# Turning the keys of both forgetting heads of a pair in one transpose, after the last scores of the pair in front

## Chip, cores and metric

The kernel runs on one core of a Trainium2 chip. The metric is the device time of one execution in microseconds (us), the median of three runs. The engines are TensorE (PE; its weight loads are shown apart as PEld), VectorE (DVE), ScalarE (ACT), GpSimd (POOL) and SyncE (SP), whose queue issues the DMAs.

## What is computed

One decoder layer over 1024 positions of width 1024 in float32. An input projection of the normalised x feeds two groups of eight heads of 64: group A, attention in a sliding window with sinks, and group B, "forgetting" attention, which is causal softmax attention with a bias from cumulated log gates. Both go through an output projection, and a feed-forward part follows.

```
xn = rmsnorm(x, attn_norm_g)
qa, ka, va, qb, kb, vb, f_logit = split(xn @ w_in)
out_a = swa_sinks_attention(rmsnorm(qa), rmsnorm(ka), va, sink_logits)
log_f = log_sigmoid(f_logit + b_forget);  c = cumsum(log_f)
# forgetting attention, for each head
sc = rmsnorm(qb) @ rmsnorm(kb).T / 8 + c[t] - c[s]      (s <= t)
out_b = softmax(sc) @ vb
x = x + concat(out_a, out_b) @ w_out
x = x + square(relu(rmsnorm(x) @ w_up)) @ w_down
```

## The kernel before

Each float32 product is done in three matmuls of float32r parts: a value is cast to a high part, and the rest is kept as a low part. Queries and keys are stacked: `q1` holds the high part of a head's query in its 64 rows and the low part in the other 64, `k1` holds the high part of the key in both row halves, and `k2` the low part of the key (`k2_of[h]`, one tile for each of the two heads of a pair, with zeros in the other rows). So the scores are two matmuls, q1 by k1 and q1 by k2.

Group B is worked in four pairs of heads, p = 0 to 3. The projection of pair p (`project_b`, eight row tiles of 24 matmuls each, tile `ps`) writes `qkb[p]`, rows of positions with columns for queries (128), keys (128) and values (128) of the two heads, and normalises them in place on POOL (`qknorm`, L239). For the scores the queries and keys have to be turned, so that positions are columns. `turn` (L299) takes four 128 x `w` blocks through PE into one PSUM tile `pt`, one of three with the tag "tr"; the same three serve the probabilities (`tpb`, L705). A half c of the positions is 512 columns.

`make_k_b` (L360) turns the keys of one head: for each half four transposes of 64 columns (`ptk`), then `k_split` (L341): two casts on ACT (L343, L344, into both row halves of k1) and one subtraction on DVE (L346, into `k2z`). For the sliding heads `make_k_a` (L352) takes 128 columns at once, two heads in one `pt`, and splits them one after the other. Queries of B are turned for both heads at once as well (`make_q_b`, `ptq`).

The pair runs in eight units u: u = 0 to 3 are head 0 and u = 4 to 7 head 1, over the query blocks in the order (0, 2, 1, 3), in which block qp has 2 qp + 2 key blocks of 128. A unit is `scores_b` (PE matmuls `spb`, a DVE reduction that adds the bias row `cb`, an exponential on ACT) and, two units later, `mix_b` (transposes `tpb`, a cast `pth` on ACT and a subtraction `ptl` on DVE for each block of 256 keys, matmuls `pvb`, an addition `mtb`). Between units `ahead(p + 1, u)` prepares the next pair: queries after u = 4, keys of head 0 and the load of its bias row after u = 5, values after u = 6, keys of head 1 after u = 7. `k1` tiles rotate through two places, `q1` tiles through four.

The order of instructions on each engine is worked out at compile time by a list scheduler over a simulated timeline, in which `prep(...)` gives high priority; projections (`fillers`) have low priority and may start only behind the scores of a certain unit (PACE, `issue_after`). After pair 3's projection its weights and the input make room for the output projection (`out_start`): `mix` tiles are loaded back from DRAM, weights `wor` are split into `wos`, and the products of the first half of `w_out` (`out_first`, tile `po`) are the fillers from then on.

Of the kernel before, what the change touches and what calls it, by code (L numbers as in the profile page):

```python
# [8 lines left out]
F32 = mybir.dt.float32  # L9
F32R = mybir.dt.float32r  # L10
# [6 lines left out]
P = 128  # L17
D = 1024
S = 1024
KT = D // P  # L20
NT = S // P
HD = 64
# [33 lines left out]
def hybrid_layer(  # L56
# [13 lines left out]
    nc = tc.nc  # L70
# [74 lines left out]
    ap2 = at.enter_context(tc.tile_pool(name="ap2", bufs=1, side="right"))  # L145
# [147 lines left out]
    def q_split(hi, lo, src, gain):  # L293
        nc.scalar.activation(hi, src, AF.Copy, scale=gain)
        nc.vector.scalar_tensor_tensor(
            out=lo, in0=src, scalar=gain, in1=hi.bitcast(F32), op0=ALU.mult, op1=ALU.subtract
        )

    def turn(x, col, w, c, name):  # L299
        pt = pa.tile([P, 512], F32, tag="tr", name=name, bufs=3)  # L300
        for j in range(4):
            nc.tensor.transpose(  # L302
                pt[:w, j * P : (j + 1) * P], x[:, 4 * c + j, col : col + w], ident
            )
        return pt
# [3 lines left out]
    def paced():  # L309
        return tc.issue_after(marks[-1]) if marks else nullcontext()  # L310

    qa, va = {}, []
    rows_of = [slice(h * HD, (h + 1) * HD) for h in range(2)]

    def tiles_q_a(g, c):
        for j in range(2):
            qa[g, j, c] = ap2.tile([P, 2, 512], F32R, tag="q1", name=f"q1a{g}{j}", bufs=4)

    def make_q_a(g, c, j):
        x, col = (((q0, 0), (q3, 0)), ((q3, P), (q3, 2 * P)))[g][j]  # L320
# [4 lines left out]
            q_split(q1[r, h, :], q1[ro, h, :], pt[r, :], gqk[r, 0:1])  # L325

    def make_q_b(x, p):
        q1 = [ap2.tile([P, S], F32R, tag="q1", name=f"q1b{p}{h}", bufs=4) for h in range(2)]
        for c in range(2):
            cs = slice(c * 512, (c + 1) * 512)  # L330
            pt = turn(x, 0, P, c, "ptq")
            for h in range(2):
                r, ro = rows_of[h], rows_of[1 - h]
                q_split(q1[h][r, cs], q1[h][ro, cs], pt[r, :], gqk[r, 1:2])
        return q1
# [3 lines left out]
    k2_of = [ap2.tile([P, S], F32R, name=f"k2z{i}") for i in range(2)]  # L339

    def k_split(k1, i, src, cs, both):  # L341
        r, ro = rows_of[i], rows_of[1 - i]
        nc.scalar.copy(k1[r, cs], src)  # L343
        nc.scalar.copy(k1[ro, cs], src)  # L344
        for rr in (r, ro) if both else (r,):
            nc.vector.tensor_tensor(  # L346
                out=k2_of[i][rr, cs], in0=src, in1=k1[r, cs].bitcast(F32), op=ALU.subtract
            )

    k1a = {}  # L350

    def make_k_a(x, col, c):  # L352
        cs = slice(c * 512, (c + 1) * 512)
        pt = turn(x, col, P, c, "ptk")
        for g in range(2):
            if c == 0:
                k1a[g] = ap2.tile([P, S], F32R, tag="k1", name=f"k1a{g}", bufs=2)
            k_split(k1a[g], g, pt[rows_of[g], :], cs, True)

    def make_k_b(x, col, p, h):  # L360
        k1 = ap2.tile([P, S], F32R, tag="k1", name=f"k1b{p}{h}", bufs=2)
        if p == 0:
            nc.gpsimd.memset(k2_of[h][rows_of[1 - h], :].bitcast(F32), 0.0)
        for c in range(2):
            cs = slice(c * 512, (c + 1) * 512)
            pt = turn(x, col + h * HD, HD, c, "ptk")
            k_split(k1, h, pt[:HD, :], cs, False)
        return k1

    def evict_pt(pt, cols):  # L370
        hi = ap2.tile([P, 512], F32R, tag="pth", name="pth", bufs=3)
# [107 lines left out]
    def start_a():  # L479
        for c in range(2):  # L480
            tiles_q_a(0, c)
        for t in range(2):
            wa1_tile(t)
        for c in range(2):
            wa1_tile(2 + c)
            with tc.issue_after(middle[-1]):
                prep(make_k_a, q0, P, c)
            prep(make_q_a, 0, c, 0)
        for g in range(2):
            va.append(split_v(q0[:, :, 256 + g * HD : 256 + (g + 1) * HD], f"va{g}"))  # L490
        prep(make_q_a, 0, 0, 1)
        for t in range(4, NT):
            wa1_tile(t)
        prep(make_q_a, 0, 1, 1)
# [128 lines left out]
    heads = {}  # L623

    def prep_q(p):
        heads[p, "q"] = make_q_b(qkb[p], p)

    def prep_k(p, h):
        heads[p, "k1", h] = make_k_b(qkb[p], P, p, h)
        if h == 0:  # L630
            load_c(p, 0)

    def load_c(p, h):
        cb = heads[p, "cb", h] = ap2.tile([P, S], F32, tag="bias", name=f"cb{p}{h}", bufs=2)
        nc.sync.dma_start(cb, c_d[2 * p + h].partition_broadcast(P))
# [96 lines left out]
    qkb = {}  # L732
# [24 lines left out]
    def ahead(p, u):  # L757
        if p > 3:
            return
        if u == 4:  # L760
            prep(prep_q, p)
        if u == 5:
            prep(prep_k, p, 0)
        if u == 6:
            prep(prep_v, p, 0)
        if u == 7:
            prep(prep_k, p, 1)

    def heads_a(g):
        for i in range(NT):  # L770
            unit(lambda: scores_a(g, i), lambda got, i=i: mix_a(got, g, i))
            if g:
                ahead(0, i)
            if (g, i) == (0, 5):
                forget_gates()
            if (g, i) in ((0, 4), (1, 0)):
                tiles_q_a(1, g)
                for j in range(2):
                    prep(make_q_a, 1, g, j)
            fill()  # L780
# [477 lines left out]
    for i in range(len(STEPS)):  # L1258
        down(i)
        if STEPS[i][0] == len(PHASES) - 1 and late:  # L1260
            name, dt, cs = late.pop(0)
# [63 lines left out]
```

## Time and profile before

| | |
|---|---|
| median of 3 runs | 1098.94 us (1097.46 to 1099.37) |
| profiled execution, its own time | 1097.17 us |
| its span, first to last instruction | 1095.5 us |
| PE busy / DVE / ACT / POOL | 99% / 71% / 52% / 33% |
| granted TensorE clock, mean | 0.999 of full |

The profile is one execution. Times in its views count from the span's start. The stretch of the forgetting heads reaches from about 160 us (first queries of pair 0) to 420 us. A matmul's duration in the trace holds its way through the array; matmuls in a row overlap, so that the distance of their starts is what one costs the queue.

### The profile page before, as it was taken

How to read it: one execution, taken by the hardware profiler on the slowest of the kernel's cores; microseconds unless marked ns; L12 is line 12 of the kernel's file. 1: busy time of each engine (PE TensorE's matmuls, PEld its weight loads, DVE VectorE, ACT ScalarE, POOL GpSimd, SP SyncE). 2: the span in 40 equal slices, each digit the busy share in tenths (PEclk: the TensorE clock that was granted, in tenths of full speed). 3: DMA queues.
4: the chain of work that ended last, by engine and by line, in shares of the span. 5: the costliest groups of instructions: out<-in, count | busy, mean ns of one | idle time of the engine just before them, and what ended most of it. 6: DMA issues, size and time to landing. Idle time of an engine off the chain costs nothing.

```text
span 1095.5 us, 15678 instructions
## 1 busy us (share of the span) xinstructions
PE 1081.4 (99%) x5557; PEld 934.0 (85%) x5557; DVE 774.7 (71%) x1327; ACT 571.6 (52%) x1013; POOL 365.2 (33%) x352
## 2 busy tenths in 40 slices
PE   9999999999998999999999999999999999999998
PEld 8999999999996888778888888888888888888886
DVE  8377677766777883898686869765665867674395
ACT  5558588676767764554545454443633433333331
POOL 5672523435433564223223232332222222222100
PEclk9999999999999999999999999999999999999999
DMA  8401212334347457663554443344898876665423
GB/s 301 146 23 52 71 38 61 115 93 149 116 154 279 156 174 280 228 214 127 195 194 177 172 165 143 144 173 144 311 391 312 306 288 230 233 224 186 174 91 115
DMA packets 96079, 195.69 MB, mean 179 GB/s; under 512 B 7376, under 2 KB 19584, under 8 KB 96000
## 3 DMA queue, kind: packets, MB, share of 16 engines
q1 hardware_dynamic: 95856, 194.66, 50.9%
q8 instruction: 44, 0.72, 0.3%
q14 instruction: 35, 0.29, 0.1%
q10 hardware_dynamic: 144, 0.02, 0.0%
HBM read 141.61 MB, written 53.04 MB: 178 GB/s over the span
## 4 chain that ended last, share of the span: by engine, by line
PE 86%; DVE 6%; DMA 5%; issue 1%; ACT 1%; POOL 1%; SPq 0%; ACTq 0%; DVEq 0%
PE pd L73 27%; PE pu L73 27%; PE ps L73 13%; PE po L73 5%; PE spb L73 3%; PE pvb L73 3%; PE tpb L705 3%; DMA xr<-in_xT_dram 1%; PE sp L73 1%; PE pv L73 1%; DMA xq<-in_x_dram 1%; PE tpa L534 1%; DMA h_d<-h 1%; PE ptk L302 1%; DVE bl L80 1%
## 5 line engine op out<-in xcount | busy, mean ns | idle before, releaser
L73 PE MATMUL pd<-hx,wx 128*128 128x512 f32 (+1 forms) x1350 | 304.9, 388 | 0.0
L73 PEld LDWEIGHTS pd<-hx,wx 128*128 128x128 f32 x1350 | 252.7, 188 | 52.2
L73 PE MATMUL pu<-bh,wu 128*128 128x512 f32 x896 | 276.5, 390 | 1.1 <-ACT wu L77 1.1
L73 PEld LDWEIGHTS pu<-bh,wu 128*128 128x128 f32 x896 | 168.2, 188 | 36.6 <-ACT wu L77 1.6
L73 PE MATMUL ps<-w,xh 128*128 128x384 f32 (+1 forms) x640 | 176.0, 345 | 0.7 <-DVE z L431 0.6
L73 PE MATMUL pu<-bl,wu 128*128 128x512 f32 x448 | 174.5, 390 | 0.6 <-DVE bl L80 0.6
L77 ACT CAST hx<-hr 128x1024 fp32r<-128x1024 f32 x56 | 58.9, 1052 | 176.6 <-PE pd L73 170.6
L80 POOL TENSOR_TENSOR wx<-wda,wx 128x1024 fp32r<-128x1024 f32 x24 | 64.5, 2686 | 196.4 <-ACT wx L77 169.1
L80 DVE TENSOR_TENSOR hx<-hr,hx 128x1024 fp32r<-128x1024 f32 x56 | 72.3, 1299 | 72.4 <-ACT hx L77 72.4
L73 PEld LDWEIGHTS ps<-w,xh 128*128 128x128 f32 x640 | 115.3, 189 | 3.1 <-DVE z L431 1.0
L73 PE MATMUL ps<-w,xl 128*128 128x384 f32 (+1 forms) x320 | 109.8, 344 | 0.0
L73 PEld LDWEIGHTS pu<-bl,wu 128*128 128x128 f32 x448 | 84.1, 188 | 19.2 <-DVE bl L80 1.0
L73 PE MATMUL po<-mix,wos 128*128 128x512 f32 x384 | 94.0, 395 | 1.0 <-ACT wos L77 0.7
L80 POOL TENSOR_TENSOR wu<-wus,wu 128x512 fp32r<-128x512 f32 x32 | 47.2, 1476 | 127.2 <-ACT wu L77 127.2
L73 PEld LDWEIGHTS po<-mix,wos 128*128 128x128 f32 x384 | 70.4, 188 | 15.5 <-ACT wos L77 1.1
L80 POOL TENSOR_TENSOR wu<-wur,wu 128x512 fp32r<-128x512 f32 x32 | 43.3, 1354 | 88.7 <-ACT wu L77 88.7
L77 ACT CAST wu<-wus 128x512 fp32r<-128x512 f32 x64 | 38.4, 618 | 58.8 <-PE pu L73 55.1
L374 DVE TENSOR_TENSOR ptl<-tpb,pth 128x512 fp32r<-128x512 f32 (+1 forms) x80 | 49.3, 631 | 25.1 <-ACT pth L373 23.1
L999 DVE TENSOR_TENSOR ht<-hb 128x512 f32<-128x512 f32 x32 | 21.8, 722 | 63.2 <-ACT hb L1054 63.2
L80 POOL TENSOR_TENSOR w<-wr,w 128x384 fp32r<-128x384 f32 (+1 forms) x47 | 51.5, 1106 | 41.2 <-ACT w L77 29.3
L77 ACT CAST wx<-wda 128x1024 fp32r<-128x1024 f32 x56 | 58.2, 1044 | 6.7 <-DMA wda<-in_w_d_dram 6.6
L73 PEld LDWEIGHTS ps<-w,xl 128*128 128x128 f32 x320 | 60.3, 188 | 1.0
(214 smaller groups left out, 1935.9 us busy)
## 6 DMA issues: line engine op xcount, KB each, us to landing
wda<-in_w_d_dram SPq DMA_DIRECT2D x34, 1024.0 KB, 9.0
hr<-hid_d SPq DMA_DIRECT2D x56, 512.0 KB, 6.0
wur<-in_w_u_dram SPq DMA_DIRECT2D x32, 512.0 KB, 4.3
hid_d<-ht SPq DMA_DIRECT2D x16, 1024.0 KB, 4.3
hid_d<-hb SPq DMA_DIRECT2D x16, 768.0 KB, 3.6
mix<-mixs_d SPq DMA_DIRECT2D x7, 1024.0 KB, 7.4
wr<-in_w_b_dram SPq DMA_DIRECT2D x32, 192.0 KB, 2.5
xr<-in_xT_dram SPq DMA_DIRECT2D x16, 256.0 KB, 4.8
```

The source lines that it names most:

```text
L73: return nc.tensor.matmul(out, lhsT, rhs, start=start, stop=stop)
L77: hi_eng.copy(hi, src)
L80: lo_eng.tensor_tensor(out=lo, in0=src, in1=hi.bitcast(F32), op=ALU.subtract)
L302: nc.tensor.transpose(pt[:w, j * P : (j + 1) * P], x[:, 4 * c + j, col : col + w], ident)
L374: nc.vector.tensor_tensor(out=lo[:, cols], in0=pt[:, cols], in1=hi[:, cols].bitcast(F32), op=ALU.subtract)
L534: nc.tensor.transpose(tp[:, hh * P : (hh + 1) * P], pts[hh // 2][:, hh % 2, c0 : c0 + P], ident)
L705: nc.tensor.transpose(tp[:, c0 : c0 + P], probs[qi][:, kb * P : (kb + 1) * P], ident)
L999: eng.tensor_tensor(out=out, in0=a, in1=b, op=ALU.subtract)
```

## The change

`make_k_b` now takes one half c and a tuple of heads. For pair 0 it is called as before, for each head by itself (after u = 5 and after u = 7). For pairs 1, 2 and 3 nothing is turned after u = 5 (only the bias row is loaded there), and after u = 7 both heads are turned together: four transposes of 128 columns for each half, then `k_split` for head 0 and for head 1 out of the same `pt`. The six places of `q1` and `k1` tiles now have a name each (q0 to q5), and the table QK says for each pair which places its two queries and its two keys take.

```diff
+    QK = ((0, 1, 4, 5), (2, 3, 0, 4), (1, 5, 2, 0), (3, 4, 1, 2))
+
+    def qk1(i, shape, name):
+        return ap2.tile([P] + shape, F32R, tag=f"q{i}", name=name, bufs=1)
...
-            qa[g, j, c] = ap2.tile([P, 2, 512], F32R, tag="q1", name=f"q1a{g}{j}", bufs=4)
+            qa[g, j, c] = qk1(2 * c + j, [2, 512], f"q1a{g}{j}")
...
-        q1 = [ap2.tile([P, S], F32R, tag="q1", name=f"q1b{p}{h}", bufs=4) for h in range(2)]
+        q1 = [qk1(QK[p][h], [S], f"q1b{p}{h}") for h in range(2)]
...
-                k1a[g] = ap2.tile([P, S], F32R, tag="k1", name=f"k1a{g}", bufs=2)
+                k1a[g] = qk1(4 + g, [S], f"k1a{g}")
...
-    def make_k_b(x, col, p, h):
-        k1 = ap2.tile([P, S], F32R, tag="k1", name=f"k1b{p}{h}", bufs=2)
-        if p == 0:
-            nc.gpsimd.memset(k2_of[h][rows_of[1 - h], :].bitcast(F32), 0.0)
-        for c in range(2):
-            cs = slice(c * 512, (c + 1) * 512)
-            pt = turn(x, col + h * HD, HD, c, "ptk")
-            k_split(k1, h, pt[:HD, :], cs, False)
-        return k1
+    def make_k_b(x, col, p, c, hs):
+        cs = slice(c * 512, (c + 1) * 512)
+        n = len(hs) * HD
+        pt = turn(x, col + hs[0] * HD if n < P else col, n, c, "ptk")
+        for i, h in enumerate(hs):
+            if c == 0:
+                heads[p, "k1", h] = qk1(QK[p][2 + h], [S], f"k1b{p}{h}")
+            if p == 0 and c == 0:
+                nc.gpsimd.memset(k2_of[h][rows_of[1 - h], :].bitcast(F32), 0.0)
+            k_split(heads[p, "k1", h], h, pt[rows_of[i], :], cs, False)
...
-    def prep_k(p, h):
-        heads[p, "k1", h] = make_k_b(qkb[p], P, p, h)
-        if h == 0:
+    def prep_k(p, u):
+        if u == 0:
             load_c(p, 0)
+        for c in range(2):
+            if p == 0:
+                make_k_b(qkb[p], P, p, c, (u,))
+            elif u:
+                make_k_b(qkb[p], P, p, c, (0, 1))
```

## Rows read from the trace of the kernel before

**Rows 1.** The page: the span, the engines' busy time (share of the span, instructions), and the granted clock in 40 equal slices.

```profile
span 1095.5 us, 15678 instructions
PE 1081.4 (99%) x5557; PEld 934.0 (85%) x5557; DVE 774.7 (71%) x1327; ACT 571.6 (52%) x1013; POOL 365.2 (33%) x352
PEclk9999999999999999999999999999999999999999
```

**Rows 2.** Waits of PE from 180 to 365 us: who waited for whom, us in total, times, longest.

```profile
PE spb L73 <- DVE nmb L663: 1.9, 4, 1.0
PE pvb L73 <- DVE mtb L722: 1.1, 1, 1.1
PE pvb L73 <- DVE ptl L374: 0.2, 1, 0.2
```

**Rows 3.** Busy time of the projection's products (tile ps) in two stretches, the last unit of pair 0 and the change from pair 2 to pair 3: length, PE, PEld, DVE, ACT, clock, share of DMA, GB/s.

```profile
220.60:233.80 13.20, 7.76 (x37) 6.35 (x37) 0.00 (x0) 0.48 (x1) 1.00 0.03 7
...
331.10:349.30 18.20, 0.00 (x0) 0.00 (x0) 0.00 (x0) 0.48 (x1) 1.00 0.86 330
```

**Rows 4.** Timeline of PE from pair 2 to pair 3: start, us, instruction, count, and in brackets the idle time before it and its releaser.

```profile
335.33 0.44 PE L73 MATMUL spb<-k1b,q1b 128*128 128x384 f32 x1 [1.00 <-DVE nmb L663]
...
337.12 0.39 PE L73 MATMUL pvb<-pth,vb 128*128 128x256 f32 x1 [1.10 <-DVE mtb L722]
...
345.65 0.28 PE L73 MATMUL pvb<-pth,vb 128*128 128x256 f32 x1
345.77 0.29 PE L73 MATMUL pvb<-ptl,vb 128*128 128x256 f32 x1
...
347.88 0.28 PE L73 MATMUL spb<-k1b,q1b 128*128 128x256 f32 x1
...
349.33 1.22 PE L73 MATMUL po<-mix,wos 128*128 128x512 f32 x4
```

**Rows 5.** DMA issues from 325 to 360 us: name, queue, count, KB each, median us from issue to landing.

```profile
mix<-mixs_d SPq DMA_DIRECT2D x4, 1024.0 KB, 8.4
```

**Rows 6.** Busy time of all engines in two stretches: length, PE, PEld, DVE, ACT, POOL, clock, share of DMA, GB/s.

```profile
331.10:349.30 18.20, 15.27 (x101) 11.79 (x99) 14.52 (x38) 13.21 (x28) 5.28 (x11) 1.00 0.86 330
345.00:350.00 5.00, 4.73 (x31) 3.67 (x31) 4.90 (x11) 4.17 (x8) 0.64 (x1) 1.00 0.51 187
```

**Rows 7.** Groups of instructions from 150 to 365 us: busy us, mean ns of one, idle time before them and what ended it.

```profile
L346 DVE TENSOR_TENSOR k2z<-ptk,k1b 64x512 fp32r<-64x512 f32 x16 | 10.8, 681 | 4.0 <-ACT k1b L344 3.8
...
L302 PE MATMUL ptk<-ident,qkb 128*64 128x128 f32 x64 | 10.0, 272 | 0.0
...
L344 ACT CAST k1b<-ptk 64x512 fp32r<-64x512 f32 x16 | 9.3, 580 | 0.2
L343 ACT CAST k1b<-ptk 64x512 fp32r<-64x512 f32 x16 | 9.3, 579 | 8.5 <-PE ptk L302 8.4
...
L302 PEld LDWEIGHTS ptk<-ident,qkb 128*64 128x64 f32 x64 | 6.9, 111 | 1.4 <-issue 0.4
...
L302 PEld LDWEIGHTS ptq<-ident,qkb 128*128 128x128 f32 x32 | 4.1, 140 | 0.7 <-POOL qkb L281 0.3
```

**Rows 8.** Timeline of PE while pair 1 is prepared: a four of query transposes and a four of key transposes with their neighbours.

```profile
217.64 0.34 PE L73 MATMUL ps<-w,xh 128*128 128x384 f32 x1
217.81 0.60 PE L302 MATMUL ptq<-ident,qkb 128*128 128x128 f32 x4
218.25 0.38 PE L705 MATMUL tpb<-ident,sb 128*128 128x128 f32 x2
...
231.29 0.60 PE L302 MATMUL ptk<-ident,qkb 128*64 128x128 f32 x4
231.64 0.37 PE L73 MATMUL pvb<-ptl,vb 128*128 128x256 f32 x1
231.85 0.28 PE L73 MATMUL pvb<-pth,vb 128*128 128x256 f32 x1
```

**Rows 9.** Timeline of ACT while the keys of the sliding heads are split.

```profile
52.06 0.56 ACT L343 CAST k1a<-ptk 64x512 fp32r<-64x512 f32 x1
...
55.99 0.58 ACT L343 CAST k1a<-ptk 64x512 fp32r<-64x512 f32 x1 [1.71 <-DVE k2z L346]
...
64.29 0.58 ACT L343 CAST k1a<-ptk 64x512 fp32r<-64x512 f32 x1 [3.00 <-DVE k2z L346]
```

**Rows 10.** Timeline of DVE in the same stretch.

```profile
54.59 1.37 DVE L346 TENSOR_TENSOR k2z<-ptk,k1a 64x512 fp32r<-64x512 f32 x2
...
57.56 1.40 DVE L346 TENSOR_TENSOR k2z<-ptk,k1a 64x512 fp32r<-64x512 f32 x2
```

**Rows 11.** Timeline of ACT from pair 2 to pair 3.

```profile
343.12 0.59 ACT L373 CAST pth<-tpb 128x512 fp32r<-128x512 f32 x1 [1.56 <-PE tpb L705]
...
345.73 0.58 ACT L343 CAST k1b<-ptk 64x512 fp32r<-64x512 f32 x1 [1.08 <-PE ptk L302]
...
348.68 0.60 ACT L77 CAST wos<-wor 128x512 fp32r<-128x512 f32 x1
349.31 0.58 ACT L343 CAST k1b<-ptk 64x512 fp32r<-64x512 f32 x1
```

**Rows 12.** Timeline of DVE in the same stretch.

```profile
344.26 0.69 DVE L374 TENSOR_TENSOR ptl<-tpb,pth 128x512 fp32r<-128x512 f32 x1
```

## Prediction, made before the change was run

> **What bounds the kernel now.** I read the page's totals first: TensorE (PE) is busy 1081.4 of 1095.5 us at the full granted clock, DVE 71%, ACT 52% [rows 1]. So a change is worth what it takes out of PE's queue, less what it adds to PE's few waits. Then the waits of PE in the change's whole stretch, 180 to 365 us: 3.2 us, all on DVE [rows 2], and by the timeline the two long ones, 1.00 and 1.10, lie at 335.33 and 337.12 [rows 4]. What is special there? At the other two places where one pair of heads follows another, products of the next projection fill PE: 37 of them, 7.8 us, in the 13.2 us of the last unit of pair 0 [rows 3]. From 331.1 to 349.3 us, where pair 3 follows pair 2, there is none [rows 3]: the projections are used up, and the first product of the output projection starts at 349.33 [rows 4], behind the loads of `mix`, four of 1 MB that take 8.4 us each [rows 5] while DMA runs at 330 GB/s [rows 6]. In this gap PE is busy 15.27 of 18.20 us [rows 6]. So time saved on PE counts in full wherever filler is queued, and inside the gap only if attention, which is all the work there, goes faster.
>
> **The turn itself.** Before, a pair's keys take 2 heads x 2 halves x 4 = 16 transposes of 64 columns; after, the last three pairs take 8 of 128 columns. 24 fall away. One lasts 272 ns [rows 7], but they are pipelined, so the price is the distance of starts. A four of ptk starts at 231.29 and the next product at 231.64; that product is followed only 0.21 later where 0.12 is the pitch of its kind (345.65 to 345.77) [rows 4, 8]. So a four takes 0.35 + 0.09 = 0.44 us. Bounds for the 24: 6 x 0.44 = 2.64 from the starts, 24 x 0.156 = 3.75 from the group's union of busy time (10.0 us over 64, [rows 7], in which overlap with the neighbours is counted). I take 2.64, since it is the queue that ends.
>
> The remaining transposes get wider weights: the load grows from 111 to 140 ns [rows 7]. If the load set the pace, 24 x 0.029 = 0.70 us would come back; but the four of ptq, whose loads are 140 ns, start at 217.81 and the next transposes at 218.25, also 0.44 [rows 8]. So 0, with 0.7 kept for the range. The Trainium skill (TensorE: Matmul & The Clock Gate, section LDWEIGHTS (loading the stationary operand)) lets a load's time grow with its columns, over 1.2 GHz, which would be 53 ns more each, an estimate of 1.3 us for the 24 by that page, and so speaks against the wide turn: by it the sum below would be 1098.2 us. The rows above show the load longer, by 29 ns, and the pitch not.
>
> **ACT and DVE.** Each head and half still has two casts of 0.58 us (k1b, both row halves) and one subtraction of 0.68 (k2z) [rows 7]. Nothing falls away and nothing is added: per pair 8 casts, 4.6 us, and 4 subtractions, 2.7 us. Only their place changes: head 0's half moves from unit 5 to unit 7, next to head 1's, which has to be behind the last scores because `k2_of[1]` is read until then. The named places add no wait that I find: those of a pair's keys are, by the table QK, of tiles read last in unit 3 of the pair in front, and those of its queries were free by unit 4 before too. They take one away: head 1's casts no longer wait for the last scores, only its subtraction does. DMAs: `load_c` is issued at the same unit as before; no queue is passed. Worth 0 on PE directly.
>
> **What the shared turn costs.** Both heads now lie in one PSUM tile, which ACT and DVE do not read at once. The keys of the sliding heads have been turned so all along: head 0's casts at 52.06, its subtractions at 54.59, and ACT then sat 1.71 us idle for them before head 1's cast at 55.99, 3.00 us at 64.29 [rows 9, 10]. The turn holds its tile from 52.06 until 57.56 + 1.40 = 58.96, 6.9 us. That tile is one of three ("tr") through which also the probabilities are turned. The Trainium skill (PSUM: Partial Sum Buffer, section PSUM bank collisions raise a hardware error) lets two engines into one bank at once where they are in different quadrants, as the two heads are; by that alone head 1's casts would not wait, and the first rival below would lose most of its chance. The rows show that this program waits, so I count the wait. Queued behind a head-1 cast on ACT are the exponentials of the last scores and the splits of weights; behind head 1's subtraction, which waits for the last scores on PE, are the reductions of pair 3's first scores on DVE, for which PE's score banks wait.
>
> At pairs 0 to 1 and 1 to 2 the longer turn is covered by the filler named above; if it were gone, a boundary would cost what it does in the gap. In the gap, ACT is busy 4.17 and DVE 4.90 of the 5 us from 345 to 350 [rows 6], head 0's turn being there already (casts at 345.73 and 349.31 [rows 11]). Head 1's first half adds 1.16 us to ACT, which has 0.83 free, and 0.68 to DVE, which has 0.10 free: 0.58 us late on the fuller engine. What is late next is either the first scores of pair 3 (347.88) or the cast of wos (348.68), and with it the first output product (349.33) [rows 4, 11]. Bounds: 0, if head 1 goes behind wos, where filler covers it; 2.3, if its four casts go in front of wos. I take 0.6, since DVE is the row that is nearest to full.
>
> **Sum.** 2.64 - 0.58 = 2.06 us less. On the profiled execution, 1097.17 (span 1095.5 and 1.7 around it), that is 1095.1; this execution lies 1.8 us under the median of the runs, and on the median the sum is 1098.94 - 2.06 = **1096.9 us**, 0.19% down. A measurement of this kernel tells about 0.2%, 2.2 us, from no change: the forecast lies on that line.
>
> **Rivals.**
> *Slots run short (slower).* In the gap two shared turns hold two "tr" tiles for up to 6.9 us each. With one tile left, a block of probabilities takes four transposes, a cast and a subtraction, 0.44 + 0.59 + 0.69 = 1.7 us [rows 8, 11, 12], and PE has 0.44 + 4 x 0.12 = 0.9 us of work in it. The last two units of pair 2 have 2 + 4 = 6 blocks: 6 x 0.8 = 4.8 us lost, 1098.94 - 2.64 + 4.8 = 1101.1. It decides from 4.8 us on, the saving and the 2.2 of the measure. For it: the two shared turns' 1.71 and 3.00 us waits. Against: filler comes at 349.33, some 4 us after the first turn. 0.14.
> *The output projection starts late (no difference).* All four casts of head 1 in front of wos: 1098.94 - 2.64 + 2.3 = 1098.6. For it: in these 5 us ACT is at 4.17. Against: before, the cast of wos went ahead of head 0's second half (348.68 and 349.31), so wos does not always come last [rows 11]. 0.17.
> *More is saved.* The order of all engines is worked out anew at compile time, and head 0's casts leave units 5 and 6 of pair 2, where DVE lets PE wait 1.0 and 1.1 us [rows 2]. Without these two waits: 1098.94 - 2.64 - 2.1 = 1094.2. Against: in the gap head 0 was turned as late as 345 already, so those units lose no DVE work. 0.19.
> *The forecast*, with 0 to 1.2 us given back (1096.3 to 1097.5): 0.50.
>
> **Chances.** The line for faster is 1098.94 x 0.998 = 1096.7, in the middle of the forecast's own span: half of it is faster, half within. Faster 0.25 + 0.19 = 0.44; slower 0.14 and a trifle from the second rival, 0.15; the rest, 0.41, within 0.2%. The range leaves out the first rival and the far end of the third: 1094.0 to 1100.0 us.
>
> **What would show it.** Right: 40 ptk transposes on qkb instead of 64, the four still 0.44 us apart, PE's busy time some 3 to 4 us down; at the first two boundaries no PE wait; head 1's casts after head 0's subtraction in the same turn; the first output product 0 to 1 us later after the last projection product. Wrong: a PE wait for k1b or k2z at any boundary; a sum of PE waits between the last projection product and the first output product above 5 us (first rival) or below 1.5 us (third); the four's pitch above 0.5 us, by which the wide loads would cost.

## The result: 0.4% slower

The changed kernel takes 1103.39 us in the median of 14 executions (1100.28 to 1106.32), the kernel before 1099.11 beside it: a ratio of 1.0040, interval 1.0029 to 1.0051, or 4.3 us more. The forecast was 2 us less. The profiled execution after has a span of 1101.4 us, before 1095.5 [rows 1].

The page after, its span and PE's busy time (share, instructions):

```profile
span 1101.4 us, 15629 instructions
PE 1081.7 (98%) x5533; PEld 932.7 (85%) x5533; DVE 778.6 (71%) x1327; ACT 570.0 (52%) x1013; POOL 361.3 (33%) x352
```

PE has 24 instructions less, as it should, and is busy as long as before. The time outside its busy time grew from 1095.5 - 1081.4 = 14.1 to 1101.4 - 1081.7 = 19.7 us: 5.6 of the 5.9 us by which the spans differ. So the loss is waiting. On whom? The waits of PE from 180 to 500 us, after (who waited for whom, us in total, times, longest):

```profile
PE po L73 <- DMA mix<-mixs_d: 4.2, 3, 2.1
PE spb L73 <- DVE nmb L678: 3.2, 3, 1.8
PE po L73 <- ACT wos L77: 2.2, 3, 1.2
...
PE po L73 <- POOL wos L80: 0.5, 2, 0.3
```

and before, where the same view has:

```profile
PE spb L73 <- DVE nmb L663: 1.9, 4, 1.0
PE pvb L73 <- DVE mtb L722: 1.4, 2, 1.1
...
PE po L73 <- ACT wos L77: 0.7, 1, 0.7
...
PE po L73 <- DMA mix<-mixs_d: 0.3, 1, 0.3
```

Products of the output projection (`po`) waited 1.0 us in all before and 6.9 after. Scores and mixes (`spb`, `tpb`, `pvb`) together wait no longer: 3.5 before and 3.5 after, with 0.2 and 0.3 in lines left out above. And where do the `po` waits lie? All of the 1.0 us before and 4.9 of the 6.9 after lie at the end of attention; of the rest, 0.5 us lie at 347 to 349 us and 1.5 at 471 to 473, where `wos` tiles are late. PE's timeline of the end of attention, after (start, us, instruction, count, and in brackets the idle time before it and its releaser):

```profile
427.31 1.66 PE L73 MATMUL po<-mix,wos 128*128 128x512 f32 x6 [1.41 <-DMA mix<-mixs_d]
431.93 1.66 PE L73 MATMUL po<-mix,wos 128*128 128x512 f32 x6 [0.77 <-DMA mix<-mixs_d]
440.15 1.67 PE L73 MATMUL po<-mix,wos 128*128 128x512 f32 x6 [2.07 <-DMA mix<-mixs_d]
448.05 2.33 PE L73 MATMUL po<-mix,wos 128*128 128x512 f32 x9 [0.69 <-ACT wos L77]
```

They lie 56 to 77 us behind the last subtraction of the keys of pair 3 (it ends at 371.4). What could connect them? The key transposes and the first scores of pair 3 in PE's timeline, after:

```profile
361.28 0.60 PE L302 MATMUL ptk<-ident,qkb 128*128 128x128 f32 x4
365.40 0.60 PE L302 MATMUL ptk<-ident,qkb 128*128 128x128 f32 x4
365.75 0.48 PE L73 MATMUL spb<-k1b,q1b 128*128 128x256 f32 x2
```

Before, the first scores of pair 3 came at 347.88 [rows 4]: they are 18 us late. PE did not stand still meanwhile; it took `po` products. Busy time of `po` in the stretches 346.4 to 367.4 and 420 to 450 us, before and then after (length, PE busy with its count, PEld, DVE, ACT, clock, DMA share, GB/s):

```profile
346.40:367.40 21.00, 11.34 (x43) 7.65 (x43) 0.00 (x0) 1.07 (x2) 1.00 0.39 125
...
420.00:450.00 30.00, 22.37 (x94) 16.93 (x93) 2.75 (x4) 1.08 (x2) 1.00 0.74 264
```

```profile
346.40:367.40 21.00, 15.89 (x65) 11.62 (x65) 0.00 (x0) 2.84 (x5) 1.00 0.45 146
...
420.00:450.00 30.00, 17.39 (x66) 11.74 (x66) 2.75 (x4) 0.56 (x1) 1.00 0.61 221
```

22 products more were taken in the first stretch, though by 420 us the lead is down to 9 (183 against 174), and 28 fewer fall into the second, the end of attention. Its first products there need the `mix` tiles 4 to 6, the outputs of pairs 0 to 2. By the code, tiles 4 and 5 are loaded into the places of tiles 0 and 1, which the filler reads to its end, and tile 6, pair 2's output, is normalised step by step between the units of pair 3. SP's queue shows the last write of tile 6 and the issue of the last of the three loads, after and then before (where the line holds two loads):

```profile
425.76 0.32 SPq L605 DMA_DIRECT2D mixs_d<-mixs  x1
...
433.31 0.37 SPq L849 DMA_DIRECT2D mix<-mixs_d  x1
```

```profile
419.33 0.33 SPq L596 DMA_DIRECT2D mixs_d<-mixs  x1
...
425.73 0.92 SPq L834 DMA_DIRECT2D mix<-mixs_d  x2
```

The write is 6.4 us late, and attention as a whole ends late: its last mix product starts at 442.98, before at 437.67 (not at 420, as the part on time and profile has it). So the filler did cover the boundary, and the loss shows 60 to 80 us later. The profiles of all twelve kernels below, before and after included, agree with that: the six executions that took 1096.6 to 1099.0 us have 85 to 100 `po` products from 420 to 450 us, the six that took 1100.0 to 1104.5 have 60 to 81. The last mix product starts by 439.1 us in the first six, and from 441.3 on in the others but one (437.4, in experiment 6). This goes together in single profiles; it does not show which is the cause.

### The profile page after: what moved, and what is told of

The parts are those of the page before. It is cut to its first block, busy times and chain, and to the rows that moved or that the text cites. A ratio compares the mean times of both kernels' runs of the same rounds, so it can differ in the third digit from the quotient of the medians.

```text
span 1101.4 us, 15629 instructions
## 1 busy us (share of the span) xinstructions
PE 1081.7 (98%) x5533; PEld 932.7 (85%) x5533; DVE 778.6 (71%) x1327; ACT 570.0 (52%) x1013; POOL 361.3 (33%) x352
## 4 chain that ended last, share of the span: by engine, by line
PE 83%; DMA 7%; DVE 6%; issue 2%; POOL 1%; ACT 1%; SPq 0%; ACTq 0%; POOLq 0%; DVEq 0%
PE pd L73 27%; PE pu L73 26%; PE ps L73 12%; PE po L73 4%; PE spb L73 3%; PE pvb L73 3%; PE tpb L720 2%; DMA wor<-in_w_o_dram 2%; PE sp L73 1%; DMA mix<-mixs_d 1%; DMA xr<-in_xT_dram 1%; PE pv L73 1%; PE tpa L543 1%; DMA xq<-in_x_dram 1%; DVE bl L80 1%
## 5 line engine op out<-in xcount | busy, mean ns | idle before, releaser
L684 ACT ACTIVATE sb<-sb,nmb 128x128 f32<-128x128 f32 (+3 forms) x64 | 49.8, 778 | 24.1 <-DVE nmb L678 23.8
```

The lines of the kernel that those rows point to most:

```text
L684: nc.scalar.activation(pr[:, :nk], pr[:, :nk], AF.Exp, scale=-1.0, bias=nm[:, c : c + 1], accum_out=dn_b[p % 2][:, h, i : i + 1] if p < 3 ...
```

## The experiments

Each ratio is to the kernel before, run beside it on the same chip, with its 95% interval. "Clock" is the mean granted TensorE clock over the executions of the kernel (each is given to 0.001); the last column is the mean of time x clock, less the same for the kernel before beside it (mean 1097.4 over 85 executions), so it estimates the difference without half-clock time (for the changed kernel 1097.4 itself is taken). It is an estimate: over the 85 executions of the kernel before, a straight line through times and clocks falls by 0.85 us for each 0.001 of clock, where time x clock takes 1.10, and the standard errors of the column are 0.3 to 0.7 us. "Ahead of the mix" alone has five executions, the others 11 to 14. Its use is explained in the fourth group.

| kernel | median us | ratio | clock | at full clock |
|---|---|---|---|---|
| after | 1103.39 | 1.0040 (1.0029 to 1.0051) | 0.9979 | +3.7 |
| names only | 1098.93 | 0.9996 (0.9985 to 1.0008) | 0.9986 | -0.2 |
| shared turn, pairs 1 and 2 | 1101.44 | 1.0017 (1.0006 to 1.0029) | 0.9985 | +2.3 |
| shared turn, pair 3 | 1101.55 | 1.0014 (1.0001 to 1.0028) | 0.9975 | +0.8 |
| both late, each by itself | 1102.50 | 1.0028 (1.0016 to 1.0040) | 0.9967 | +1.5 |
| shared turn ahead of the mix | 1103.34 | 1.0042 (1.0029 to 1.0054) | 0.9962 | +1.7 |
| casts first | 1099.01 | 1.0001 (0.9992 to 1.0009) | 0.9982 | -0.5 |
| casts first, ahead of the mix | 1096.48 | **0.9979 (0.9970 to 0.9988)** | 0.9980 | -3.1 |
| each by itself, ahead of the mix | 1101.02 | 1.0010 (1.0001 to 1.0019) | 0.9995 | +2.8 |
| after, split 6 in one unit | 1100.98 | 1.0017 (1.0008 to 1.0027) | 0.9985 | +1.7 |
| casts first, ahead, split 6 | 1097.30 | 0.9978 (0.9969 to 0.9986) | 0.9984 | -2.0 |

**1. The names alone.** The changed kernel with each head's keys turned as before.

```diff
         for c in range(2):
-            if p == 0:
-                make_k_b(qkb[p], P, p, c, (u,))
-            elif u:
-                make_k_b(qkb[p], P, p, c, (0, 1))
+            make_k_b(qkb[p], P, p, c, (u,))
```

> The named places q0 to q5 with the table QK, but the keys of every head turned by themselves, head 0 after unit 5 and head 1 after unit 7, as before the change. Its lists of instructions are, engine by engine, in the order of the kernel before. Theory (the late third turn): the names do nothing, time as before, 1099 us, and no more than 0.2% from it. Rival (the named places cost): the 4 us of the change come with the names, 1102 to 1104 us.

Measured 0.9996, no difference, and the order of instructions on every engine is that of before. The named places are out of it; the rest is the shared turn.

**2. Which pairs.** The shared turn for pairs 1 and 2 only, and for pair 3 only (the condition `p == 0` becomes `p not in (1, 2)` or `p not in (3,)`).

> The changed kernel, but the keys of pair 3 are turned head by head as before (after unit 5 and unit 7 of pair 2); pairs 1 and 2 keep the shared turn. Theory (only the third turn is late, in the stretch that has no projection left): 16 transposes fall away at 0.11 us, 1.8 us less than before, 1097.3 us (0.998 of before), the first key transposes of pair 3 at about 345 us and its first scores before 350 us. Rival (every shared turn costs, since both heads' casts and subtractions take turns on one PSUM tile): two thirds of the loss stay, 1101 to 1102 us.

> The changed kernel, but only pair 3 has the shared turn after unit 7; pairs 1 and 2 are turned head by head as before. Theory: all of the loss and a third of the saving, 1099.1 + 4.3 + 1.8 = 1105 us, first scores of pair 3 some 18 us later than before. Rival (every shared turn costs the same): a third of the loss, 1100 to 1101 us.

My theory after the result was that only the gap in front of pair 3 costs. It fell: 1.0017 and 1.0014, both slower, each with somewhat less than half of the loss (at full clock 2.3 and 0.8 of 3.7 us, near the two thirds and one third of the rival that every shared turn costs the same). Pairs 1 and 2 lose although projection products fill PE at both of their boundaries. With the shared turn for them alone, the first key transposes of pair 3 come in time, at 347.23, but those of head 1 at 365.03 (before 358.10), the last mix product at 441.32, and 67 `po` products from 420 to 450 us: its loss, too, shows at the end of attention.

**3. The place apart from the sharing.** Both heads behind the last scores, as in the changed kernel, but each by itself, with transposes of 64 columns into its own PSUM tile.

```diff
-        for c in range(2):
-            if p == 0:
-                make_k_b(qkb[p], P, p, c, (u,))
-            elif u:
-                make_k_b(qkb[p], P, p, c, (0, 1))
+        for h in (0, 1):
+            for c in range(2):
+                if p == 0 and h == u or p and u:
+                    make_k_b(qkb[p], P, p, c, (h,))
```

> The changed kernel, but both heads of pairs 1 to 3, though still after unit 7, are turned each by itself: four transposes of 64 columns into a PSUM tile of its own for each head and half. So the place is that of the change and the sharing is gone. Theory (the place costs, not the sharing): as slow as the change and the 24 transposes on top, 1103.4 + 2.6 = 1106 us, first scores of pair 3 after 360 us. Rival (the shared PSUM tile costs): back to the time of before, 1099 us.

Measured 1.0028, between the two expectations: the later place by itself costs, 3.1 us as measured and 1.5 at full clock, with no saved transposes to set against it. The change saves them and loses more, so the sharing costs as well.

**4. Place and handovers.** A handover is the passing of a tile from one engine that reads it to the next. Two more edits to the changed kernel, alone and together. The first sets the shared turn ahead of the mix of unit 5 (which the changed kernel issues behind the scores of unit 7, in front of the turn):

```diff
-    def unit(score, mix):
+    def unit(score, mix, between=None):
         got = prep(score)
+        if between:
+            between()
         pend.append(lambda: mix(got))
...
-        if u == 7:
+        if u == 7 and p == 0:
             prep(prep_k, p, 1)
...
-            unit(lambda: scores_b(p, qp, h), lambda got, qp=qp, h=h: mix_b(got, p, qp, h))
+            unit(lambda: scores_b(p, qp, h), lambda got, qp=qp, h=h: mix_b(got, p, qp, h),
+                 (lambda: prep(prep_k, p + 1, 1)) if u == 7 and p < 3 else None)
```

> The changed kernel, but the shared turn of pairs 1 to 3 is written between the scores of unit 7 and the mix of unit 5, so that it has priority over that mix; nothing else differs. Theory A (the turn stands in line behind the mixes for the three PSUM tiles, and the next pair's scores stand still for 9 us at each boundary while the projections are used up): the key transposes of pair 1 come some 3 us sooner (about 234 instead of 237 us), those of pair 3 well before 355 us, and most of the loss goes, 1099 to 1100.5 us. Theory B (the two heads' taking turns on one PSUM tile is the loss): no change against the changed kernel, 1103 us.

The second makes all four casts of a shared tile first and then both subtractions, so that the tile changes hands between ACT and DVE once and not three times:

```diff
-            k_split(heads[p, "k1", h], h, pt[rows_of[i], :], cs, False)
+            for rr in (rows_of[h], rows_of[1 - h]):
+                nc.scalar.copy(heads[p, "k1", h][rr, cs], pt[rows_of[i], :])
+        for i, h in enumerate(hs):
+            nc.vector.tensor_tensor(
+                out=k2_of[h][rows_of[h], cs], in0=pt[rows_of[i], :],
+                in1=heads[p, "k1", h][rows_of[h], cs].bitcast(F32), op=ALU.subtract)
```

> The changed kernel, but of a shared turn all four casts come first and then both subtractions, so that ACT and DVE hand the PSUM tile over once instead of three times; place and transposes are those of the change. Theory B (taking turns on one tile costs): two handovers fewer for each of six turns, the two tiles come free 1 to 2 us sooner, 1101 us. Theory A (place): head 0's subtraction comes 1.2 us later, all else equal, 1103 to 1104 us.

Both together:

> Both edits: the shared turn has priority over the mix of unit 5, and all four casts come before both subtractions. If place (A) and handovers (B) both cost, this is the fastest of the shared turns, below before by part of the 2.6 us of transposes: 1097 to 1099 us. If only A holds, as the run without casts first, 1099 to 1100.5; if only B, as the run with casts first alone, 1101.

Casts first regains the whole loss (1.0001). Ahead of the mix alone regains nothing (1.0042). Together they give 0.9979, 2.3 us under before (1.3 to 3.3 by the interval) and faster than both kernels. Pair 3's keys, ACT's casts and DVE's subtractions after (start, us, instruction, count):

```profile
361.91 0.58 ACT L350 CAST k1b<-ptk 64x512 fp32r<-64x512 f32 x1
362.51 0.58 ACT L351 CAST k1b<-ptk 64x512 fp32r<-64x512 f32 x1
363.11 0.59 ACT L886 COPY pc<-po 128x512 f32<-128x512 f32 x1
363.59 0.62 ACT L77 CAST wos<-wor 128x512 fp32r<-128x512 f32 x1
364.24 0.58 ACT L350 CAST k1b<-ptk 64x512 fp32r<-64x512 f32 x1
...
370.08 0.58 ACT L351 CAST k1b<-ptk 64x512 fp32r<-64x512 f32 x1
```

```profile
363.12 0.68 DVE L353 TENSOR_TENSOR k2z<-ptk,k1b 64x512 fp32r<-64x512 f32 x1 [0.37 <-ACT k1b L351]
365.45 0.69 DVE L353 TENSOR_TENSOR k2z<-ptk,k1b 64x512 fp32r<-64x512 f32 x1 [1.65 <-ACT k1b L351]
...
370.69 0.69 DVE L353 TENSOR_TENSOR k2z<-ptk,k1b 64x512 fp32r<-64x512 f32 x1 [1.04 <-ACT k1b L351]
```

The last subtraction ends at 371.38, 10.1 us after the first transpose (361.28). With casts first, and with both edits, in the same two views:

```profile
356.19 2.38 ACT L378 CAST k1b<-ptk 64x512 fp32r<-64x512 f32 x4
358.46 0.37 ACT L742 COPY mtb<-pvb 64x256 f32<-64x256 f32 x1
358.86 2.36 ACT L378 CAST k1b<-ptk 64x512 fp32r<-64x512 f32 x4
```

```profile
361.25 1.39 DVE L380 TENSOR_TENSOR k2z<-ptk,k1b 64x512 fp32r<-64x512 f32 x2
```

```profile
347.70 4.76 ACT L378 CAST k1b<-ptk 64x512 fp32r<-64x512 f32 x8
```

```profile
352.49 1.39 DVE L380 TENSOR_TENSOR k2z<-ptk,k1b 64x512 fp32r<-64x512 f32 x2 [0.98 <-ACT k1b L378]
```

The turn of pair 3 then takes 7.7 us (354.95 to 362.64) and, with both edits, 7.2 (346.72 to 353.88). In the handover order none of ACT's casts is shown to wait for a subtraction; the compile-time order puts other work in between (between 362.51 and 364.24 a copy and a cast of the output projection), and each such step stretches the turn. So what the two edits show is the worth of the order of reads, not a wait at the handovers. And the turn of pair 3 not only gets shorter, it starts sooner: its first transposes come at 361.28 after, at 354.95 with casts first in the same place of the program, at 353.05 ahead of the mix and at 346.72 with both edits. How much of the gain is the shorter turn and how much the earlier start, these runs do not separate. At pair 1 the turn takes 7.9 us after and 7.7 with casts first, which is nothing, and how the loss of pairs 1 and 2 comes about stays open.

The filler shows the difference too. `po` from 420 to 450 us, casts first and then both edits (columns as above), beside 66 products after and 94 before:

```profile
420.00:450.00 30.00, 21.18 (x88) 15.85 (x88) 2.75 (x4) 1.17 (x2) 1.00 0.71 259
```

```profile
420.00:450.00 30.00, 23.36 (x100) 17.98 (x99) 2.66 (x4) 1.18 (x2) 1.00 0.71 263
```

and the waits of PE from 180 to 500 us with both edits:

```profile
PE po L73 <- ACT wos L77: 1.9, 2, 1.5
...
PE po L73 <- POOL wos L80: 0.3, 1, 0.3
```

No `po` product waits for `mix` any more.

Why, then, does the place regain nothing as long as the turn hands its tile over three times? The clock column offers an answer, from five executions. That kernel ran at a mean granted clock of 0.9962, the lowest of all; its profile has PE waits of 3.15 us at 342.86 and 1.48 at 345.21, in the gap before pair 3, and the clock there at its half level. Two windows of it (length, PE, PEld, DVE, ACT, POOL, granted clock, DMA share, GB/s):

```profile
342.00:345.00 3.00, 0.87 (x3) 0.50 (x3) 0.97 (x2) 0.37 (x1) 0.00 (x0) 0.50 1.05 339
345.00:348.00 3.00, 2.79 (x11) 2.60 (x12) 2.08 (x6) 2.30 (x5) 1.28 (x1) 0.50 0.90 311
```

At full clock it is +1.7 against +3.7 after, by which the place gives back 2.0 us (standard error 0.8) and the clock takes them. With casts first the place gives 2.6 (from -0.5 to -3.1). And casts first gives 4.2 late (3.7 to -0.5) and 4.8 ahead of the mix (1.7 to -3.1). By this estimate the two effects add up, within what 5 to 14 executions and a clock given to 0.001 can tell. Without it, the worth of the place is shown with casts first alone (0.9979 against 1.0001).

**5. The place without sharing.**

```diff
# to the kernel "ahead of the mix": each head by itself, in a PSUM tile of its own
-        for c in range(2):
-            if p == 0:
-                make_k_b(qkb[p], P, p, c, (u,))
-            elif u:
-                make_k_b(qkb[p], P, p, c, (0, 1))
+        for h in (0, 1):
+            for c in range(2):
+                if p == 0 and h == u or p and u:
+                    make_k_b(qkb[p], P, p, c, (h,))
```

> Both heads behind the last scores, each turned by itself in a tile of its own (64 columns), and these turns set ahead of the mix of unit 5 of the pair in front. Nothing is saved on transposes and no head waits for the other in a tile. If what e5 lost (3.1 us) is the late place alone, and short turns make it worth while to go ahead of the mix (as e10 against e9, 2.5 us), this runs at before's time: 1098.5 to 1100. Rival: the place behind the last scores costs whatever stands around it, and e10 was an arrangement that happened to fall well; then it stays where e5 was, 1102 to 1103.

Measured 1.0010 (1.0001 to 1.0019), against 1.0028 late: on the clock as it ran, 2.0 us better, between the expectations. But at full clock it is +2.8 against +1.5: by this estimate it gains by the clock (0.9995 against 0.9967) and not by shorter work. So a gain of the place is found for the shared turn alone, and turning both heads behind the last scores costs some 1 to 3 us, wherever exactly it is put, when no transposes are saved.

**6. The end of attention.** When is the `mix` tile ready that the last products wait for? It is split in two halves, one in each of two units. Both halves in one unit for tile 6:

```diff
+        if e == 6:
+            return [load, lambda: [make(0), make(1)]]
         return [load, lambda: make(0), lambda: make(1)]
```

> The changed kernel, but the splitting of pair 2's mixed output (e = 6), which is done in two units, has both halves in one: its last write, and with it the load of mix 6 for which PE waited 2.07 us at 440 us, comes one unit sooner. Theory (the loss is paid at the end, where the lagging attention delivers mix 6 late): the waits of PE for mix between 425 and 445 us, 4.2 us in all in the changed kernel, fall to about 2, 1101.5 us. Rival (the end is bound by the attention's own chain, and a shorter wait for mix 6 only moves on): within 0.5 us of the changed kernel, 1103 us.

> e10 (short shared turns ahead of the mix) and the two halves of the split of mix tile 6 in one unit. If the late split of tile 6 is a way in which the lag is paid, and e10 has no lag, nothing is left for it to win: 1096 to 1097. If the split costs by itself, whatever the lag, it wins as in e8: 1094 to 1095.

In the changed kernel it wins 0.23% (1.0040 to 1.0017), 2.5 us as measured and 2.0 at full clock. With both edits of experiment 4 it wins nothing (0.9978 against 0.9979). Both times are near those expected of the lag: a late `mix` tile costs only where attention is late. But the win did not come as expected. In the changed kernel with this edit the last write of tile 6 is at 429.27 and its load is issued at 433.77, no sooner than after (425.76 and 433.31). What went away are the waits for the first two loads (1.41 and 0.77 us, now none), which are issued from 418.43 on instead of 420.30 and 422.45, and the last mix product starts at 437.41 instead of 442.98. The order was laid anew, so this experiment does not show that tile 6 was the limit.

## Why the prediction was wrong

**The bound and the saved transposes: right.** 40 `ptk` transposes on `qkb` are left. The groups of the line after (busy us, mean ns of one):

```profile
L302 PE MATMUL ptk<-ident,qkb 128*128 128x128 f32 x24 | 3.6, 272 | 0.0
...
L302 PEld LDWEIGHTS ptk<-ident,qkb 128*128 128x128 f32 x24 | 2.9, 140 | 0.1
L302 PE MATMUL ptk<-ident,qkb 128*64 128x128 f32 x16 | 2.4, 272 | 0.0
```

Their starts sum to 3.63 us, before to 5.51 (worked out from the starts of PE's instructions): 1.9 us less for the transposes alone, where the term was 2.64 with their followers. The kernel with both edits gains 2.3 as measured and 3.1 at full clock, which brackets it.

**The wide loads: right.** The load is 140 ns, as predicted, and a four still takes 0.60 us from first start to last end (361.28), as it does with 64 columns [rows 8]. The distance of starts is 92 ns in the mean of the 24 wide transposes and 86 for the 64 narrow ones before, which comes to some 0.15 us. The estimate of 1.3 us for the wide loads, worked out from the Trainium skill (TensorE: Matmul & The Clock Gate, section LDWEIGHTS (loading the stationary operand)), is not borne out: the load grew by 29 ns and not 53, and the pitch hardly at all.

**The names: right**, by experiment 1.

**The shared turn: the step that failed.** "At pairs 0 to 1 and 1 to 2 the longer turn is covered by the filler" and "0.58 us late on the fuller engine" were meant as its whole price. Both judge a delay by whether PE waits there and then. The price was about 6 us: by the estimates at full clock, 4.2 for taking casts and subtractions in turn and some 2 for the place behind the mix, of which the saved transposes give back 2 to 2.6. Three things went wrong:

- Cover was taken as free. `po` products are a fixed stock, so that filler taken while scores are late can be missing where the last work has nothing else beside it: 22 more were taken from 346 to 367 us, and from 427 to 449 us their waits grew from 1.0 to 4.9 us. That the one pays for the other is argued, not shown: of the lead 9 products are left at 420 us, some 2 us of PE's time (21 in a row take 4.95 us from 355.02), and with the shared turn for pairs 1 and 2 alone (a lead of 3) the end is as empty. What the slower profiles share, but for one, is that attention ends late.
- The place was read from the old order. The prediction had the third turn start where head 0 was turned before, at 345 us. It starts at 361.28. The whole turn now stands behind the mix of unit 5 and takes its PSUM tiles from the same three: set ahead of that mix, it starts 8.2 us sooner.
- The handover was counted as ACT's and DVE's busy time in 5 us. It was known from the sliding heads that ACT and DVE take turns on the tile [rows 9, 10], and the remedy, all casts first, was not seen. The Trainium skill (PSUM: Partial Sum Buffer, section PSUM bank collisions raise a hardware error) allows two engines in different quadrants of one bank at once; no run here tried it.

**The rivals.** The first one, slots run short, had the right sign, and a time (1101.1) 2.3 us under what was measured, but another mechanism: its 4.8 us of PE waits in the gap did not come. The waits of PE from 331 to 349 us sum to 3.5 us after (1.75 and 0.96 the longest) and to 2.9 before. None of the signs that I had named for "wrong" came: no PE wait for `k1b` or `k2z`, the sum of waits between 1.5 and 5, the pitch of a four under 0.5. They watched the stretch of the change, and the loss was elsewhere. But two of the signs for "right" failed. PE's busy time was to fall by 3 to 4 us and did not (1081.7 against 1081.4; the clocks of the two executions, 0.998 and 0.999, make up about 1 us of that, an estimate). And the first output product was to come 0 to 1 us later behind the last projection product; it came 20.6 us behind it (326.98 to 347.54) where it had come 18.8 (330.53 to 349.33), 1.8 us later.

**Open.** Every edit lays the compile-time order anew, so some of any single difference may be the order's luck; that casts first gains about as much in either place (4.2 and 4.8 us at full clock) speaks against luck there. Not settled are how pairs 1 and 2 lose, through which waits the order of reads costs its 4 us, and why the place gives nothing at full clock where heads do not share a tile.

## What to carry to other kernels

A delay that filler hides need not be free: here PE hardly waited longer at the boundary (3.5 us against 2.9), and most of the loss appeared 60 to 80 us later. Look up what the last work of the kernel will have beside it, and price the delay there. When two heads share one PSUM tile, let one engine finish all its reads of it before the other begins; here that order of eight casts and four subtractions a pair was worth more than the saved transposes. A step that waits for the last scores may belong ahead of older work in the queue, if its successors are what is next on the path; here that was worth something with casts first and is not shown for heads turned apart.

## What the hardware showed

**The granted clock can fall behind a wait.** Windows of 3 us in the gap before pair 3, after and then before (length, PE busy with its count, PEld, DVE, ACT, POOL, granted clock, DMA share, GB/s):

```profile
333.00:336.00 3.00, 1.25 (x8) 0.83 (x7) 2.78 (x8) 2.52 (x6) 0.00 (x1) 1.00 1.01 414
336.00:339.00 3.00, 2.90 (x14) 2.08 (x15) 1.65 (x8) 1.63 (x4) 1.27 (x2) 0.71 0.99 358
339.00:342.00 3.00, 3.00 (x19) 2.54 (x18) 0.88 (x3) 1.68 (x4) 1.93 (x3) 0.72 0.99 393
```

```profile
333.00:336.00 3.00, 2.00 (x13) 1.46 (x11) 2.94 (x8) 2.85 (x8) 0.34 (x2) 1.00 1.03 418
336.00:339.00 3.00, 1.90 (x13) 1.56 (x13) 2.35 (x10) 1.50 (x4) 0.59 (x1) 1.00 1.04 422
```

After, PE was busy 1.25 of 3 us, with one wait of 1.75 us, and the clock was at its half level (1.2 of 2.4 GHz) in part of the next 6 us: scores of 128x512 took 0.63 us there and 0.40 before it:

```profile
333.37 0.40 PE L73 MATMUL spb<-k2z,q1b 128*128 128x512 f32 x1
...
339.57 0.63 PE L73 MATMUL spb<-k2z,q1b 128*128 128x512 f32 x1
```

In this execution of the kernel before, with two shorter waits and 1.90 to 2.00 us of work in 3, the clock stayed. Nor does every long wait bring it down: in the same execution after, PE waited 2.07 us before 440.15 (busy 0.93 of 3 us from 438 to 441), and the clock is 1.00 there and in the 9 us behind. What decides is not shown here. The mean clock of the other executions of the kernel before goes from 0.996 to 1.000, and their times follow it: of 35 run beside the first experiments, the four at 0.996 took 1101.8 us in the mean, the five at 1.000 took 1097.6. Over all 85 executions of it beside the experiments the clock goes with about half of the variance of the times (correlation -0.74). The profile that I worked from, at 0.999, was one of the lucky ones, and a difference of 2 us between two kernels has to be read beside it: of the changed kernel's loss of 4.3 us, an estimated 3.7 are left at full clock.

**Small writes land late behind large loads.** The 64 KB writes of mixed heads, issued from 300 to 325 us and from 333 to 340 us, after (count, KB each, median us from issue to landing):

```profile
mix_d<-mtb SPq DMA_DIRECT2D x3, 64.0 KB, 2.6
```

```profile
mix_d<-mtb SPq DMA_DIRECT2D x2, 64.0 KB, 10.8
```

In the first stretch DMA moved 141 GB/s in the mean, in the second 379, with loads of `mix`, x and weights under way. The kernel before shows the same (10.6 us), so it is not the cause of the loss, but a write that lands 8 us later holds its `mtb` tile as much longer: ahead of the mix, one of ACT's copies into `mtb` waits 2.4 us for such a write.
